# The first half of the second conv matrix by seven block products for eight, its stage ordered by the list scheduler

## Chip, cores, metric

One core of one Trainium2 chip runs the whole kernel. The metric is the device time in microseconds (us), the median of the runs; one more execution was taken with the hardware profiler, and all views of the trace are of that one.

## What is computed

One decoder layer on 256 tokens behind 16 meta tokens (D_MODEL 2048, all float32):

```python
u = rms_norm(h, g_pre_mix)
z_pool, v_conv, g_conv, gate_a, gate_b = split(u @ w_in)
y_a = causal_multiscale_pool(z_pool, w_pool_grp, pool_scale) @ w_pool_out
y_b = conformer_conv(v_conv, g_conv, w_dw, b_dw, conv_ln_g, conv_ln_b) @ w_conv_out
m = sigmoid(gate_a) * y_a + sigmoid(gate_b) * y_b
h = h + rms_norm(m @ w_o, g_post_mix)
f = square(relu(rms_norm(h, g_pre_mlp) @ w_up)) @ w_down
h = h + rms_norm(f, g_post_mlp)
```

The change lies in `@ w_conv_out`: (256 x 1024) by (1024 x 2048).

## The kernel before

**Products in three parts.** Every float32 operand is split into a rounded high part (fp32r, a copy on ScalarE) and the rest (a subtraction on VectorE), and a product is the sum of high x high, high x low and low x high. A weight block is 512 rows by 512 columns, 1 MiB: `raw` (three rooms, filled from the queue of SyncE), `hi` and `lo` (three rooms each). One *block product* is 128 tokens by such a block: 4 row groups x 3 parts = 12 matmuls of 128x512.

**The stages around the change**, in order: gates (L831), the group map of the pool (`acc_grp`), the pool projection (`acc_po`, w_pool_out, eight blocks), the conv projection (`acc_co`, w_conv_out, eight blocks), and the products of w_o. Pool and conv projection run through `project_t`: for each of four column blocks n, two row blocks kc, two token halves t. `fetch` keeps the split two blocks ahead: it opens the next block of the list `stream` (its load goes to SyncE's queue when the room `raw` is free, which is when the split of three blocks earlier is done), splits it when TensorE has left the parts of three blocks earlier, and hands out the oldest.

**Work behind the pool stage.** `pending` is a list of VectorE work with costs, drained between products; `late` holds ScalarE work sent off at the next fetch. In the pool stage they run the LayerNorm's end and swish: `c` ends up as the activations S, and `s_act` gets their high and low parts.

**Behind each conv column block** (`evac_conv`, L938, L939): the accumulated block times sg[1] (the sigmoid of gate_b), plus sg[0] (already times the pool's result), into one of four rooms `mts`; later `feature_steps` transposes it on TensorE (`mt`, L920), and ScalarE and VectorE write the parts into `m` (L924, L927); for the first two column blocks ScalarE also copies it to `A` (L929), from which `sums_of_m` (L952 to L955) makes sums for w_o.

**The w_o stage** already does seven block products for eight in places, and its items are ordered by the class `Plan`: each item names its engine, a cost, what it reads and writes; TensorE's and SyncE's items keep the order written out by hand (`STEPS`, which begins "P2 X02 P1 P5 P3 P6"), the others go by the earliest start, then by the time at which TensorE's planned order needs them. What comes out is a fixed program order for every engine. `early_sums` holds two sums of w_o blocks, made by four transfers on GpSimd's queue (two plain, two that add to what is there, L906), issued when the pool stage is over; P5, P6, P4 and P7 use them. P3's weight block is loaded into a room that sg[1] held (tag s1) and added to the first early sum (L1134). L1118 and L1123 are the split in this stage.

Of the kernel before, what the change touches and what calls it, by code (L numbers as in the profile page):

```python
# [15 lines left out]
P = 128  # L16
CK = 4
# [98 lines left out]
def hybrid_block(ctx: ExitStack, tc: tile.TileContext, ins: dict, out: bass.AP):  # L116
# [127 lines left out]
    def part_tile(tag, n, standing=False):  # L244

        key = f"{tag}{n % 3}"
        room = ready.pop(key) if key in ready else part_room(key, f"{tag}_{n}")
        place = 2 if standing and tag == "hi" else 1
        shift = (place - 1 - 3 * KEYS.index(key)) % 4 * LINE
        return room[:, shift:shift + CK * CW]  # L250

    def open_chunk(loads=None):

        n = at["n"]
        at["n"] += 1
        src, (rows, width) = stream[n]
        raw = raws.tile([P, CK * CW], F32, tag="raw", name=f"raw_{n}")
        hi, lo = (part_tile(tag, at["parts"], n in standing_chunks) for tag in ("hi", "lo"))
        at["parts"] += 1
        flat, (raw, hi, lo) = raw, (t.rearrange("p (k c) -> p k c", k=rows) for t in (raw, hi, lo))  # L260
        if n < FIRST:
            dst = raw.rearrange("p k (h c) -> p k h c", h=2)
            for load in loads or [(slice(i, i + 2), BOTH, nc.sync) for i in range(0, rows, 2)]:
                if callable(load):
                    load()
                    continue
                sl, halves_, queue = load
                for k in range(sl.start, sl.stop):
                    queue.dma_start(dst[:, k, halves_], src[:, k, halves_])
        else:  # L270
            nc.sync.dma_start(raw, src)
        pieces = rows if n < FIRST else 4 if n == FIRST else 1
        k = rows // pieces

        def high(sl, cs):
            nc.scalar.copy(hi[:, sl, cs], raw[:, sl, cs])  # L276

        def low(sl, cs):
            nc.vector.tensor_sub(lo[:, sl, cs], raw[:, sl, cs], f32(hi[:, sl, cs]))  # L279
# [10 lines left out]
        opened.append((hi, lo, todo, flat))  # L290

    def split_pieces(c):
        while opened[c][2]:
# [529 lines left out]
    def block(n):  # L823
        return slice(n * CW, (n + 1) * CW)
# [60 lines left out]
    pending += [(0, ln_out), (0, ln_act)]  # L885

    def evac_pool(n):
        def f(t, acc):
# [11 lines left out]
    def source_o(key):  # L900
        return columns(w_o, key[0] * CK, CK, key[1] * CW)[0][0]

    early_sums = big.tile([P, 2, CK * CW], F32, tag="k8", bufs=2, name="early_sums")
    for keys, op in ((((0, 0), (0, 1)), {}), (((0, 1), (1, 1)), {"accum_op": ALU.add})):
        for e, key in enumerate(keys):
            nc.gpsimd.dma_start(early_sums[:, e].rearrange("p (k c) -> p k c", k=CK),  # L906
                                source_o(key), **op)

    pairs_room = big.tile([P, 3, 2 * T], F32, tag="ux", name="pairs")
    m = big.tile([P, LINE + KD * 2 * T], F32R, tag="um", name="m")[:, LINE:].rearrange(  # L910
        "p (k a t) -> p k a t", k=KD, a=2)

    def feature_steps(n, t, mt):

        box = {}

        def turn():
            box["pt"] = pt = misc_tile(f"mt_{n}_{t}").rearrange("p (k c) -> p k c", k=CK)
            for i in range(CK):
                nc.tensor.transpose(pt[:, i, :], mt[:, i * P:(i + 1) * P], ident)  # L920
        dst = m[:, n * CK:(n + 1) * CK, :, t * P:(t + 1) * P]

        def high():
            nc.scalar.copy(dst[:, :, 0, :], box["pt"])  # L924

        def low():
            nc.vector.tensor_sub(dst[:, :, 1, :], box["pt"], f32(dst[:, :, 0, :]))  # L927
            if n < 2:
                nc.scalar.copy(A[:, t, n], box["pt"])  # L929
        return turn, high, low  # L930

    def mt_of(n, t):
        return mts[:, (n * NT + t) % (CC // CW * 2), :]

    def evac_conv(n):
        def f(t, acc):
            mt = mt_of(n, t)
            nc.vector.tensor_mul(mt, acc, sg[1][:, t, block(n)])  # L938
            nc.vector.tensor_add(mt, mt, sg[0][:, t, block(n)])  # L939
            blocks.extend(feature_steps(n, t, mt))  # L940
        return f

    def s_act_of(k):
        return ln["out"][:, k, :, :]


    A = big.tile([P, NT, 2, CK, P], F32, tag="a", name="A")

    def sums_of_m():

        a11, a12, a21, a22 = (A[:, t, h] for t in range(2) for h in range(2))
# [5 lines left out]
    mts = big.tile([P, CC // CW * 2, CW], F32, tag="c", name="mts")  # L957
    blocks = []
# [7 lines left out]
    later = {}  # L966

    class Norm:

# [50 lines left out]


    plan = Plan()
    HALVES = ("hi", "lo")
# [199 lines left out]

    def m_last(t):

        f_pe, f_hi, f_lo = feature_steps(NB - 1, t, mt_of(NB - 1, t))
# [846 lines left out]
```

## Time and profile before

| | |
|---|---|
| median of 3 runs | 1184.38 us (1184.14 to 1184.66) |
| profiled execution | 1184.32 us |
| its span, first to last instruction | 1182.6 us |
| granted TensorE clock | 0.997 |
| busy: TensorE / VectorE / ScalarE / GpSimd | 1172.7 / 1027.6 / 679.6 / 45.0 us |
| pool projection on TensorE | 333.19 to 376.74 us |
| conv projection on TensorE | 376.74 to 422.99 us |

PE is TensorE, DVE VectorE, ACT ScalarE, POOL GpSimd, SP SyncE. The chain lists, in order of time, what the end of the span hung on: start, us, engine, tile, line, and how many instructions. In the groups, x8 | 18.3, 2289 means eight instructions, 18.3 us in all, 2289 ns each; behind the next bar stands the idle time of the engine just ahead of them and what ended it. A timeline row is start, us, engine, line, operation, out<-in. A row of windows is the stretch, its length, busy time and instructions of the engine asked for, then the granted clock, the DMA engines' busy share, and GB/s.

### The profile page before, as it was taken

The page shows a single profiled execution, that of the slowest core. Times are in us where ns is not written, and L with a number is a line of the kernel's source. Part 1 is how long each engine was busy: PE and PEld are TensorE (multiplying, and loading weights), DVE is VectorE, ACT ScalarE, POOL GpSimd, SP SyncE. Part 2 cuts the span into 40 slices and gives each one's busy share as a digit, 9 for nine tenths or more (in the row PEclk, how much of TensorE's full clock was granted, in tenths as well). Part 3 has the DMA queues.
Part 4 walks back from the last instruction along what each step waited for, and adds up shares of the span by engine and source line. Part 5 has one row for each costly group of instructions (what it writes and reads, how often), then busy time and mean ns, then how long its engine had stood idle before and what let it go on. Part 6 is the DMA issues. An engine that isn't in the chain of part 4 may idle for free.

```text
span 1182.6 us, 15774 instructions
## 1 busy us (share of the span) xinstructions
PE 1172.7 (99%) x6351; PEld 1018.9 (86%) x6351; DVE 1027.6 (87%) x1095; ACT 679.6 (57%) x690; POOL 45.0 (4%) x51
## 2 busy tenths in 40 slices
PE   9999999999999999999999999999999999999997
PEld 9999988888888888898888888888888888888886
DVE  6899978999766799987998988989989989889865
ACT  6533344444584465756566766666656667666642
POOL 1000000000000001000001001000000010010000
PEclk9999999999999999999999999999999999999998
DMA  8655565655647967859869898988998898998861
GB/s 295 214 178 179 182 204 184 196 195 184 208 143 268 265 215 221 290 168 317 248 213 249 228 288 220 269 269 226 281 293 215 267 279 229 282 241 239 303 214 72
DMA packets 177882, 272.91 MB, mean 231 GB/s; under 512 B 4657, under 2 KB 92913, under 8 KB 176912
## 3 DMA queue, kind: packets, MB, share of 16 engines
q1 hardware_dynamic: 160176, 235.88, 59.0%
q0 software_dynamic: 16736, 34.76, 16.2%
q10 hardware_dynamic: 896, 1.25, 0.3%
q8 instruction: 50, 0.82, 0.3%
q14 instruction: 24, 0.20, 0.1%
HBM read 267.68 MB, written 4.19 MB: 230 GB/s over the span
## 4 chain that ended last, share of the span: by engine, by line
PE 99%; DVE 0%; DVEq 0%; issue 0%; ACT 0%; ACTq 0%
PE bank_u L498 18%; PE acc_gate L802 15%; PE bank_a L1787 10%; PE bank_u L504 9%; PE acc_up L1787 8%; PE bank_b L1787 7%; PE o_c L1170 6%; PE acc_z L493 4%; PE acc_co L802 4%; PE acc_po L802 4%; PE acc_v L493 3%; PE acc_g L493 3%; PE acc_vg L493 2%; PE acc_up L498 1%; PE bank_u L1787 1%; PE o_b L1170 1%
## 5 line engine op out<-in xcount | busy, mean ns | idle before, releaser
L498 PE MATMUL bank_u<-m,hi 128*128 128x512 f32 x960 | 329.4, 390 | 0.0
L504 PE MATMUL bank_u<-m,lo 128*128 128x256 f32 x960 | 265.5, 277 | 0.0
L276 ACT CAST hi<-raw 128x2048 fp32r<-128x2048 f32 (+2 forms) x94 | 151.0, 1620 | 188.1 <-PE acc_gate L802 64.0
L498 PEld LDWEIGHTS bank_u<-m,hi 128*128 128x128 f32 x960 | 180.2, 188 | 37.9
L279 DVE TENSOR_TENSOR lo<-raw,hi 128x2048 fp32r<-128x2048 f32 (+2 forms) x94 | 180.0, 1925 | 34.6 <-ACT hi L276 34.1
L1570 DVE TENSOR_TENSOR lo<-raw_m,hi 128x2048 fp32r<-128x2048 f32 x70 | 160.3, 2290 | 31.6 <-ACT hi L1566 31.5
L504 PEld LDWEIGHTS bank_u<-m,lo 128*128 128x128 f32 x960 | 180.3, 188 | 1.4
L1566 ACT CAST hi<-raw_m 128x2048 fp32r<-128x2048 f32 x70 | 133.9, 1912 | 73.7 <-DVE raw_m L1583 21.3
L802 PE MATMUL acc_gate<-hi,u_um 128*128 128x512 f32 x416 | 131.1, 389 | 0.0
L559 DVE SCALAR_TENSOR_TENSOR c<-a,taps,c 128x256 f32<-128x256 f32 x240 | 115.7, 484 | 6.8
L1787 PE MATMUL bank_a<-hi,forms 128*128 128x512 f32 (+1 forms) x288 | 93.5, 386 | 0.0
L802 PEld LDWEIGHTS acc_gate<-hi,u_um 128*128 128x128 f32 x416 | 78.1, 188 | 16.1
L802 PE MATMUL acc_gate<-lo,u_um 128*128 128x512 f32 x208 | 80.9, 389 | 0.0
L1570 DVE TENSOR_TENSOR lo<-raw_a,hi 128x2048 fp32r<-128x2048 f32 x29 | 66.4, 2290 | 10.8 <-ACT hi L1566 10.7
L1566 ACT CAST hi<-raw_a 128x2048 fp32r<-128x2048 f32 x29 | 55.4, 1910 | 35.4 <-PE bank_u L498 13.2
L1566 ACT CAST hi<-raw_c 128x2048 fp32r<-128x2048 f32 x27 | 51.5, 1909 | 27.2 <-PE bank_u L498 12.4
L1570 DVE TENSOR_TENSOR lo<-raw_c,hi 128x2048 fp32r<-128x2048 f32 x27 | 61.8, 2289 | 5.7 <-ACT hi L1566 5.6
L1787 PEld LDWEIGHTS bank_a<-hi,forms 128*128 128x128 f32 x288 | 53.9, 188 | 11.0
L1570 DVE TENSOR_TENSOR fourth_pair<-raw_m,fourth_pair 128x2048 fp32r<-128x2048 f32 x26 | 59.5, 2288 | 4.4 <-ACT fourth_pair L1566 4.4
L1650 ACT COPY half<-bank_u 128x256 f32<-128x256 f32 x60 | 22.2, 370 | 66.0 <-PE bank_u L504 66.0
L1787 PE MATMUL acc_up<-hi,forms 128*128 128x512 f32 x176 | 57.4, 390 | 0.0
L1787 PE MATMUL bank_a<-lo,forms 128*128 128x512 f32 (+1 forms) x144 | 55.6, 386 | 0.0
(419 smaller groups left out, 2265.0 us busy)
## 6 DMA issues: line engine op xcount, KB each, us to landing
raw<-in_w_in_dram SPq DMA_DIRECT2D x52, 1024.0 KB, 5.1
raw_m<-in_w_down_dram SPq DMA_DIRECT2D x38, 1024.0 KB, 7.0
raw_m<-in_w_down_dram POOLq DMA_DIRECT2D x22, 1024.0 KB, 10.6
raw_a<-in_w_up_dram SPq DMA_DIRECT2D x20, 1024.0 KB, 6.4
raw_c<-in_w_up_dram SPq DMA_DIRECT2D x19, 1024.0 KB, 6.9
raw_m<-in_w_up_dram SPq DMA_DIRECT2D x19, 1024.0 KB, 6.9
raw_a<-in_w_down_dram SPq DMA_DIRECT2D x13, 1024.0 KB, 7.3
raw_c<-in_w_down_dram SPq DMA_DIRECT2D x13, 1024.0 KB, 7.3
```

What stands on the lines that cost most here:

```text
L276: nc.scalar.copy(hi[:, sl, cs], raw[:, sl, cs])
L279: nc.vector.tensor_sub(lo[:, sl, cs], raw[:, sl, cs], f32(hi[:, sl, cs]))
L493: nc.tensor.matmul(acc, w[:, k[0], cs], act[:, k[1], a, off:], start=first and n == 0, stop=last and n == 2)
L498: nc.tensor.matmul(acc.rearrange("p (a t) -> p a t", a=2)[:, :, ts], hi[:, k[0], cs], act[:, k[1], :, off + ts.start:off + ts.stop], start ...
L504: nc.tensor.matmul(acc[:, :T], lo[:, k[0], cs], act[:, k[1], 0, off:], start=False, stop=stop, skip_group_check=True)
L559: nc.vector.scalar_tensor_tensor(c, conv["a"][:, q, i:i + T], taps[:, q, i:i + 1], c, op0=ALU.mult, op1=ALU.add)
L802: nc.tensor.matmul(acc, act(kk)[:, a_, ts_], w_[:, k, :], start=kk == 0 and n == 0, stop=kk == nk - 1 and n == 2)
L1170: nc.tensor.matmul(acc, form(k, a_), box[w_][:, k, :], start=start and k == 0 and n == 0, stop=stop and k == CK - 1 and n == 2, skip_group ...
L1566: nc.scalar.copy(box["hi"], raw)
L1570: nc.vector.tensor_sub(box["lo"], raw, f32(box["hi"]))
L1650: nc.scalar.copy(box[j], accs[j][:, :T])
L1787: nc.tensor.matmul(acc, forms[h][:, f, k, a_, :], box[w_][:, k, cs], start=start and k == 0 and n == 0, stop=stop and k == KH - 1 and n == ...
```

## The change

**Seven for eight.** For the first two column blocks (n = 0, 1) the matrix is a 2 x 2 grid of blocks Bkn, the activations a 2 x 2 grid of halves Ath (tokens t, channels h), and four results are made by seven block products on sums. Products 1, 2 and 4 take the plain activations from `s_act`; 5, 6, 7 and 3 take sums of them (`conv_sums`, four passes over c in place, then a high and a low part each, `conv_high`, `conv_low`). On the weight side 1, 2 and 3 take plain blocks; 5 takes B11 + B12, 6 that plus B22, 7 B12 + B22, and 4 the sum of all four. These sums are made in `conv_wide`, in the room of u (tag um), by eight transfers on GpSimd's queue, issued ahead of the pool stage: three plain, five that add; B22 is added to the room of 5 on VectorE, behind the split of 5.

**Column blocks 2 and 3** stay plain: X20, X21, X30, X31 (column block, row block), each for token half a and b. So eight products more.

**Order.** The stage is no longer `project_t` but a second `Plan`, `cplan`. TensorE's order is `ORDER`; f00 is the transposition of column block 0, token half 0; `sums` is sums_of_m. The first two blocks ("1", "5") are still opened and split by the pool stage's fetch. Each of eleven weight entries is split (before: eight). The four results of the seven products are put together from one bank `ch`, to which 1, 6, 7 and 4 are added one after the other, with ScalarE copies of it in between (`keep`), and two more banks; each joined result then takes the two gate passes as before. `mts` gets its room (tag c) only when all forms have been read from c.

**What moves.** `early_sums` is loaded behind product 3, since the forms of 7 and 3 hold its room (tag k8) until then; `m` and `A` get their rooms inside the stage.

```diff
@@ the list of weight blocks
-    for w, nk in ((w_pool_out, KP), (w_conv_out, KC)):
-        for n in range(NB):
-            stream += columns(w, 0, nk, n * CW)
+    for n in range(NB):
+        stream += columns(w_pool_out, 0, KP, n * CW)
...
+    CONV = ("1", "5", "6", "2", "7", "X20", "4", "3", "X21", "X30", "X31")
+    CONV_LOADS = {"1": (0, 0), "2": (1, 0), "3": (1, 1)}
+    ORDER = "1 5 6 2 7 X20a f00 X20b 4 3 f11 X21a f01 X21b f10 sums X30a X30b f20 f21 X31a X31b"
...
+    def open_room(key):
+        raw = conv_raw(key)
+        hi, lo = (part_tile(tag, at["parts"]) for tag in ("hi", "lo"))
...
+        more = conv_raw("3") if key == "5" else None
+        def f():
+            nc.scalar.copy(hi, raw)
+            nc.vector.tensor_sub(lo, raw, f32(hi))
+            if more is not None:
+                nc.vector.tensor_add(raw, raw, more)
...
@@ ahead of the pool stage
-        pending[0:0] = [a_[0], b_[0], FETCH, a_[1], b_[1], FETCH, a_[2], b_[2]]
+        pending[0:0] = [a_[0], b_[0], FETCH, a_[1], b_[1], FETCH, a_[2], b_[2],
+                        (2.4, conv_sums), FETCH] + [(0.6, conv_low(key)) for key in "56"]
...
+    conv_wide = big.tile([P, 3, CK * CW], F32, tag="um", name="conv_wide")
+    sums_ = {"6": ((0, 0), (0, 1)), "7": ((0, 1), (1, 1)), "4": ((0, 0), (0, 1), (1, 1), (1, 0))}
+    for i in range(4):
+        for n, (key, blocks_) in enumerate(sums_.items()):
+            conv_rooms[key] = conv_wide[:, n]
+            if i < len(blocks_):
+                add_into(conv_rooms[key], conv_block(*blocks_[i]), ALU.add if i else None)
...
+    FORM_C = {"5": (0, 0, (1, 0)), "6": (0, 1, (1, 1)), "7": (1, 0, (0, 0)), "3": (1, 1, (0, 1))}
...
@@ behind the pool stage
-    for keys, op in ((((0, 0), (0, 1)), {}), (((0, 1), (1, 1)), {"accum_op": ALU.add})):
-        for e, key in enumerate(keys):
-            nc.gpsimd.dma_start(early_sums[:, e].rearrange("p (k c) -> p k c", k=CK),
-                                source_o(key), **op)
...
-    for n in range(NB):
-        after += blocks + [sums_of_m] * (n == 2)
-        blocks.clear()
-        project_t(s_act_of, KC, evac_conv(n), f"co{n}")
+    cplan = Plan()
+    BANK_C = {"1": "ch", "6": "ch", "7": "ch", "4": "ch", "2": "w2", "5": "w3", "3": "w3"}
...
+    def load_c(e, src, rows=CK, ahead=False):
+        r = n_loads[0] % 3
+        n_loads[0] += 1
+        loads_c[e] = f"raw{r}"
...
+        cplan.add("SP", 0.0 if ahead else 3.1, f, writes=(f"raw{r}",), late=0.0 if ahead else 3.0)
...
+        cplan.add("ACT", 1.83, high, reads=(name,), writes=(f"hi{q}",))
+        cplan.add("DVE", 2.22, low, reads=(name, f"hi{q}"), writes=(f"lo{q}",))
...
+    cplan.add("ACT", 0.0, place_forms, writes=("S7", "S3"))
+    for key in "73":
+        form_parts(key)
...
+    cplan.add("ACT", 0.0, place_mts, writes=["c"] + [f"h{i}" for i in range(4)])
...
+    def keep(n, t, bank):
+        cplan.add("ACT", 0.5, lambda: nc.scalar.copy(mt_of(n, t), conv_banks[bank]),
+                  reads=(bank,), writes=(h_of(n, t),))
...
+        if unit == "1":
+            keep(0, 0, "ch")
+        elif unit == "5":
+            keep(0, 1, "w3")
+        elif unit == "6":
+            keep(1, 0, "ch")
+            cplan.add("ACT", 0.0, place_a, writes=("S5", "S6", "Aroom"))
+        elif unit == "2":
+            joined(0, 0, nc.vector.tensor_add, lambda: conv_banks["w2"], lambda: mt_of(0, 0),
+                   ("w2", h_of(0, 0)))
+        elif unit == "7":
+            keep(1, 1, "ch")
...
+        elif unit == "3":
...
+            cplan.add("ACT", 0.0, place_early, writes=("S7", "S3", "early0", "early1"))
+            early_load(0, (0, 0), None)
+            early_load(1, (0, 1), None)
+            early_load(0, (0, 1), ALU.add)
+            early_load(1, (1, 1), ALU.add)
+        elif unit == "4":
+            gate_conv(0, 1, "ch")
...
+    cplan.emit()
```

More of the change, by code (lines that the diff above doesn't have):

```diff
@@ new lines, in gate_conv, with joined @@
+    def gate_conv(n, t, bank=None):
+        h = h_of(n, t)
+        cplan.add("DVE", 0.62, lambda: nc.vector.tensor_mul(
+            mt_of(n, t), conv_banks[bank] if bank else mt_of(n, t), sg[1][:, t, block(n)]),
+            reads=(bank,) if bank else (h,), writes=(h,))
+        cplan.add("DVE", 0.62, lambda: nc.vector.tensor_add(
+            mt_of(n, t), mt_of(n, t), sg[0][:, t, block(n)]), reads=(h,), writes=(h,))
+    def joined(n, t, op, a_, b_, names):
+        cplan.add("DVE", 0.62, lambda: op(mt_of(n, t), a_(), b_()), reads=names,
+                  writes=(h_of(n, t),))
+        gate_conv(n, t)
@@ new lines, in hybrid_block, with features, steps @@
+    turns = [0]
+    def features(n, t):
+        assert {"mroom", "Aroom"} <= set(cplan.writer)
+        box, bank, j = {}, f"mt{turns[0] % 2}", f"m{n}{t}"
+        turns[0] += 1
+        def steps():
+            if "s" not in box:
+                box["s"] = feature_steps(n, t, mt_of(n, t))
+            return box["s"]
+        cplan.add("PE", 0.45, lambda: steps()[0](), reads=(h_of(n, t),), writes=(bank,))
+        cplan.add("ACT", 0.53, lambda: steps()[1](), reads=(bank, "mroom"), writes=(j,))
+        cplan.add("DVE", 0.62, lambda: steps()[2](), reads=(bank, j), writes=(j + "l",))
+        if n < 2:
+            cplan.add("ACT", 0.5, lambda: nc.scalar.copy(A_[0][:, t, n], box["s"][3]["pt"]),
+                      reads=(bank, "Aroom"), writes=(f"A{t}{n}",))
@@ new lines, in place_early @@
+    def place_early():
+        later["early"] = big.tile([P, 2, CK * CW], F32, tag="k8", bufs=2, name="early_sums")
+    entry_of = {key: e for e, key in enumerate(CONV)}
+    used = {}
+    for u_, unit in enumerate(UNITS):
+        used[entry_of[unit.rstrip("ab")]] = u_
+    W_O = (len(CONV), len(CONV) + 1)
+    BEHIND = {}
+    for item in ORDER.split():
+        if item in UNITS:
+            last_unit = item
+            BEHIND[item] = []
+        else:
+            BEHIND[last_unit].append(item)
@@ new lines, in hybrid_block, with after_split @@
+    loaded = ["2", "X20", "X21", "X30", "X31"]
+    wanted_c = [(entry_of[key], conv_block(*(CONV_LOADS.get(key) or (int(key[2]), int(key[1]))))[0])
+                for key in loaded] + [(W_O[i], stream[at["n"] + len(CONV) - ahead_c + i][0])
+                                      for i in range(2)]
+    n_loads[0] = 2
+    load_c(*wanted_c.pop(0), ahead=True)
+    loads_c[entry_of["1"]], loads_c["3"] = "raw0", "raw1"
+    split_done = ahead_c
+    x_banks = []
+    def after_split(e):
+        if wanted_c and e in (entry_of[k] for k in ("2", "3", "X20", "X21", "X30", "X31")):
+            load_c(*wanted_c.pop(0))
@@ L965, in hybrid_block @@
+    while split_done < len(CONV) + 2:
+        split_c(split_done, "w_o")
+        split_done += 1
+    cplan.emit()
+    m = later["m"]
+    early_sums = later["early"]
+    for e in W_O:
+        opened.append((*conv_parts[e], [], flats[e]))
+    at["parts"] = first_c + len(CONV) + 2
+    at["n"] += len(CONV) - ahead_c + 2
     og = big.tile([P, NT, D], F32, tag="k8", bufs=2, name="og")
-    later = {}
+    A = A_[0]
     class Norm:
@@ L1022, in hybrid_block @@
     plan = Plan()
-    HALVES = ("hi", "lo")
     SA1, SA2, SA3, SA4 = ((1, 0), (1, 1), (0, 0), (0, 1))
```

178 lines of the change are left out of this document (155 added, 23 removed).

## The prediction

> **What bounds the kernel now.** I read the page first (busy times, then the chain that ended last), then the chain between 333 and 462 us, then VectorE's groups and windows there, then the DMA queues.
>
> ```profile
> span 1182.6 us, 15774 instructions
> PE 1172.7 (99%) x6351; PEld 1018.9 (86%) x6351; DVE 1027.6 (87%) x1095; ACT 679.6 (57%) x690; POOL 45.0 (4%) x51
> PE 99%; DVE 0%; DVEq 0%; issue 0%; ACT 0%; ACTq 0%
> ```
>
> TensorE is the bound: it is busy for 99% of the span and the chain runs through it for 99%. A matmul left out shortens the kernel only while nothing makes TensorE wait; VectorE, at 87%, is the engine that could.
>
> ```profile
> 333.19 43.55 PE acc_po L802 x192
> 376.74 16.32 PE acc_co L802 x72
> 393.06 0.87 PE mt L920 x8
> ...
> 422.99 2.73 PE o_c L1170 x12
> 432.05 2.72 PE o_a L1170 x12
> 434.77 5.44 PE o_c L1170 x24
> ```
>
> Three stages follow each other without a gap: the pool projection, the conv projection (376.74 to 422.99, 46.25 us: 192 matmuls and, three times, eight transposes), and w_o. In w_o, P2 stands at 422.99, P1 at 432.05, P5 at 434.77 and P3 behind it at 437.5.
>
> **What it saves.** A block product is 12 matmuls, 2.73 us (16.32/6). The stage had 16 and gets 7 + 8 = 15; the six transposes stay. If nothing waits, the saving is 2.7 us, 0.23% of the time: this is the ceiling, and any stop of TensorE comes off it. About 0.2%, 2.4 us, is what a measurement here can tell from no change.
>
> **What it adds on VectorE.**
>
> ```profile
> L279 DVE TENSOR_TENSOR lo<-raw,hi 128x2048 fp32r<-128x2048 f32 x8 | 18.3, 2289 | 7.6 <-ACT hi L276 7.6
> L939 DVE TENSOR_TENSOR mts<-mts,sg 128x512 f32<-128x512 f32 x7 | 4.8, 692 | 0.2
> 376.74:422.99 46.25, 33.67 (x33) 1.00 0.83 250
> 422.99:462.00 39.01, 37.50 (x29) 1.00 0.87 284
> 373.28 2.29 DVE L279 TENSOR_TENSOR lo<-raw,hi 128x2048 fp32r<-128x2048 f32 x1 [3.15 <-ACT hi L276]
> 375.49 0.69 DVE L889 TENSOR_TENSOR sg<-acc_po,sg 128x512 f32<-128x512 f32 x1
> 371.33 1.91 ACT L276 CAST hi<-raw 128x2048 fp32r<-128x2048 f32 x1 [3.53 <-PE acc_po L802]
> 393.53 0.58 ACT L924 CAST m<-mt 128x512 fp32r<-128x512 f32 x1 [3.96 <-PE mt L920]
> ```
>
> A split costs ScalarE 1.9 and VectorE 2.2 us (start to start, 373.28 to 375.49); a pass over 128x512 costs VectorE some 0.65. Behind the pool stage VectorE now gets eleven splits for eight (24.2), sixteen gate passes (10.4), six low parts (3.9), the sums of m (2.6), and new: two low parts of forms (1.3), three joins (1.95), the tail of B22's addition (1) and the last two pool evacuations (1.3): 46 to 47 us, against 33.67 before. TensorE needs 15 x 2.73 + 2.6 = 43.6. So VectorE turns from a quarter idle into as long as the stage; what it can't finish goes into w_o, where it is busy 37.5 of 39.0 us. The four sums of A (2.5) and the low parts of forms 5 and 6 lie in the pool stage, where VectorE waits 3.15 us before single splits: they cost nothing, and delay the split of the last pool block by under 3 us, which TensorE needs 4 us later.
>
> **The stop at product "6".** ScalarE and VectorE work in program order. "5" is split first; behind its subtraction VectorE adds B22 to the same room; only then "6" can be cast; and TensorE may add "6" to the chain's bank only when ScalarE has kept the bank in mts, whose room is that of c, which the forms 7 and 3 must have left. From the rows: cast of "5" 371.33, subtraction 373.28 to 375.5, addition to 377.7, cast of "6" to 379.6, subtraction to 381.9, two form subtractions to 383.2, the copy (0.58) to 383.8. TensorE gets there at 376.74 + 2 x 2.73 = 382.2. A stop of 1.6 us, then, even if all data are there. The planner counts neither the addition nor the pool evacuations, since both were issued ahead of it.
>
> **What it adds on the queues.** Eight transfers of 1 MiB go to the GpSimd queue as soon as u's room is free: three plain, five that add. Nothing else stands on it there. The early sums of w_o (two and two) move from the start of the stage to behind product "3".
>
> ```profile
> 325.00 0.39 PE L802 MATMUL acc_gate<-hi,u_um 128*128 128x512 f32 x1
> 358.26 34.03 SPq L271 DMA_DIRECT2D raw<-in_w_conv_out_dram  x8
> 377.04 1.57 POOL L906 DMA_DIRECT2D early_sums<-in_w_o_dram  x2 [371.21 <-PE acc_po L802]
> 384.98 1.30 POOL L906 DMA_DIRECT2D early_sums<-in_w_o_dram  x1 [6.37 <-DMA early_sums<-in_w_o_dram]
> 388.50 1.28 POOL L906 DMA_DIRECT2D early_sums<-in_w_o_dram  x1 [2.22 <-DMA early_sums<-in_w_o_dram]
> early_sums<-in_w_o_dram POOLq DMA_DIRECT2D x1, 1024.0 KB, 7.4
> early_sums<-in_w_o_dram POOLq DMA_DIRECT2D x1, 1024.0 KB, 13.5
> early_sums<-in_w_o_dram POOLq DMA_DIRECT2D x1, 1024.0 KB, 18.0
> 381.04 0.37 SPq L271 DMA_DIRECT2D raw<-in_w_conv_out_dram  x1
> raw<-in_w_conv_out_dram SPq DMA_DIRECT2D x1, 1024.0 KB, 5.1
> raw<-in_w_conv_out_dram SPq DMA_DIRECT2D x1, 1024.0 KB, 8.7
> 386.48 0.37 SPq L271 DMA_DIRECT2D raw<-in_w_conv_out_dram  x1
> raw<-in_w_conv_out_dram SPq DMA_DIRECT2D x1, 1024.0 KB, 13.3
> 391.92 0.37 SPq L271 DMA_DIRECT2D raw<-in_w_conv_out_dram  x1
> raw<-in_w_conv_out_dram SPq DMA_DIRECT2D x1, 1024.0 KB, 14.9
> ```
>
> The last column is the time to landing of the load issued in that window. A weight load alone takes 5.1. The loads issued at 381.04, 386.48 and 391.92 landed at 389.7, 399.8 and 406.8; the two adding transfers at 398.5 and 406.5. So while adding transfers are on, one weight block and one adding block pass per (406.7 - 389.7)/2 = 8.5 us, where the stage eats a block per 5.4.
>
> Put on the pool stage: the plain three, shared with loads, end near 332, 338 and 344 (some 5.8 each, two blocks at 2.9); the first three adding ones near 352, 360 and 368. The load of "1", issued at 358.26, stands behind the last pool block (which I put at 364.5) and lands near 370.7 instead of 363.4. Its split ends on VectorE near 374.8, in time for 376.74; the split of "5" then ends at 377.0, the addition (B22 landed at 376.3) at 379.2 instead of 377.7. The stop at "6" grows by 1.5 to 3.2 us (my value: the pair price was measured on these same queues; bounds 1.6, if the loads keep their 5.1, and some 5, if every pair takes the 10.1 of the first one).
>
> The sum of "4" adds three times in a chain, each after the last has landed: two more of 8.5 and two issues, landed near 392. It is cast at the earliest behind product "2"; TensorE needs "4" at 376.74 + 7 x 2.73 + 0.4 + 3.2 = 399.4, so the cast by 395. Cost nothing, 3 us spare; past that every us is TensorE's, and it stands in ScalarE's queue before the copy behind "7", the split of "3" and the features of block (0,0).
>
> For one such transfer the Trainium skill (DMA: Bandwidth & Descriptors, Anatomy of one DMA) gives 2.0 us plus bytes over 436 GB/s, 4.4 us for 1 MiB. Eight in a row would then be done by 361 and the stop at "6" would stay at 1.6; the rows above, 7.4 to 18.0, speak against it.
>
> **The stop in w_o.**
>
> ```profile
> 423.03 1.92 ACT L1118 CAST hi<-raw_o 128x2048 fp32r<-128x2048 f32 x1 [3.00 <-PE acc_co L802]
> 424.98 2.29 DVE L1123 TENSOR_TENSOR lo<-raw_o,hi 128x2048 fp32r<-128x2048 f32 x1
> 431.19 2.28 DVE L1134 TENSOR_TENSOR early_sums<-early_sums,raw_o 128x2048 f32<-128x2048 f32 x1
> 434.07 2.29 DVE L1123 TENSOR_TENSOR lo<-raw_o,hi 128x2048 fp32r<-128x2048 f32 x1
> ```
>
> P3's split ends at 436.3, 1.2 us ahead of TensorE: the tightest place. Its block is loaded when the last gate has left sg's room, and added to the first early sum at 431.19. With the stop of 3.2 the conv stage ends at 376.74 + 43.6 + 3.2 = 423.5, 0.5 later than before. VectorE, full since 381, does the last gate product near 426.4 instead of 424.3. The early transfers start behind "3", at 405; the plain ones land near 413 and 418, the adding ones near 427 and 435 (before: 398.5 and 406.5). P3's load of 426.4 shares with the last of these and lands near 435.3; addition to 437.5, a form to 438.1, the split to 440.4. TensorE wants it at 437.5 + 0.5 = 438.0: a stop of 2.4. Bounds: none, if that load takes 5.1 and lands at 431.5; 5, if it takes the 13 to 15 us of the loads above.
>
> **The sum.** -2.7 + 3.2 + 2.4 = +2.9 us. The profiled execution took 1184.32 for its span of 1182.6 and the median is 1184.38, so I say 1187.2. Everything behind w_o is as before.
>
> **The rivals.**
> - *Only the chain at "6" stops.* Loads land as alone: -2.7 + 1.6, and up to 1 for VectorE's backlog: 1183.2 to 1184.2, within 0.2%. For it: in 325 to 377 the DMA engines now have slack. Against: eight transfers come into it. 0.27.
> - *Nothing stops: the faster side.* If VectorE puts the two form subtractions into its waits before the split of "6" and the copy of the chain's bank leaves before 382.2, and the blocks land alone, the 2.7 stays: 1181.6. It decides at whether "6" starts at 382.2. Against: the order on VectorE is by due time, which puts the split of "6" first. 0.08.
> - *The sum of "4" lands late.* At 10 us a pair the chain lands at 397 to 400; ScalarE and VectorE stand still behind that cast, and since VectorE has no slack it costs 2 to 5 on top: 1189 to 1193. 0.13.
> - *The plan does not say what is run.* The planner names the room of X21's load as that of B22. If the pool of rooms really turned in that order, the load would wait for the split of "3" near 402, land 5 to 8 later, and X21 (wanted at 408) start at 412 to 414: 1191 to 1194. 0.06. For it: the names; against: two other rooms are free earlier.
> - *The clock drops behind a stop.*
>
> ```profile
> 1.12 3.35 PE idle L394 x14
> 5.82 0.67 PE idle L394 x6
> ```
>
> The first fourteen of these small matmuls took 239 ns each, six later ones 112. If a stop of over 3 us brings this back for 3.35 us, half of it, 1.7, is added: 1189. In these windows the granted clock is 1.00 and there is no stop, so the trace can't tell. The Trainium skill (TensorE: Matmul & The Clock Gate, HAM oscillation) has the limit at idle gaps of about 3.4 us. 0.05.
>
> **Chances and range.** Forecast 0.41. Slower: the forecast and the last three, 0.65, less some 0.04 for the forecast's lower half, which falls under 2.4: 0.61. Faster 0.08. Within 0.2%: 0.31. The range takes in the quiet rival and its neighbour, from 1182.0, and reaches over the late "4" and the room, to 1194.0; the likeliest case's own range, by the bounds of both stops, is 1183 to 1191.
>
> **What would show it.** Right: a TensorE gap of 2 to 4 us before the third product of the conv stage, released by ScalarE's copy of the chain's bank; weight loads of 8 us and more between 344 and 410; VectorE over 95% busy from 381 to 425; a second gap at the fifth product of w_o, behind the addition to the first early sum. Wrong: loads of 5 us in the pool stage (then the first stop is 1.6 and the second is gone); no gap at "6"; or the longest gap at "4" or X21.

## The result, and the profile after

The changed kernel takes 1187.92 us (median of seven executions, 1186.58 to 1188.65) against 1184.55 for the kernel before (seven, 1183.91 to 1184.72): ratio 1.0029, 95% interval 1.0017 to 1.0041. It is slower, by 3.4 us. Its profiled execution took 1186.58, the shortest of the seven; so the profile below accounts for 2.3 of the 3.4 us, and the rest has to be looked for elsewhere.

The page after, the share of the chain, and TensorE's waits from the pool stage on (engine, line, what ended the wait; us in total, times, longest):

```profile
span 1184.9 us, 15791 instructions
PE 1171.5 (99%) x6339; PEld 1016.4 (86%) x6339; DVE 1042.9 (88%) x1110; ACT 689.6 (58%) x701; POOL 53.9 (5%) x59
PE 92%; DVE 3%; DMA 3%; ACT 1%; issue 0%; DVEq 0%; ACTq 0%
PE acc_co_chain L1205 <- ACT mts L1095: 2.6, 1, 2.6
PE o_c L1459 <- DVE lo L1412: 0.6, 1, 0.6
PE acc_po L844 <- DVE lo L293: 0.6, 1, 0.6
```

Twelve matmuls fewer, and the chain, which ran through TensorE for 99%, now leaves it for two long stretches (338.5 to 385.5 and 400.0 to 439.7). TensorE's three waits lie in these; the chain shows what it passes through ahead of each:

```profile
342.80 19.30 DMA raw<-in_w_pool_out_dram
...
366.45 10.41 DMA raw_conv<-in_w_conv_out_dram
376.96 2.30 DVE conv_wide L318
379.36 1.91 ACT hi L1054
381.30 1.07 DVE lo L1058
383.51 1.30 DVE conv_forms L962 x2
384.83 0.59 ACT mts L1095
385.47 3.02 PE acc_co_chain L1205 x12
...
401.92 2.29 DVE lo L1058
...
425.89 0.61 DVE mts L1100
426.52 7.95 DMA raw_o<-in_w_o_dram
434.56 2.29 DVE early_sums L1423
437.45 2.21 DVE lo L1412
439.71 2.81 PE o_c L1459 x11
```

First place, the pool stage: the load of its last-but-one block takes 19.3 us, and TensorE stands still until 366.5. Second, product "6": B22's block lands at 376.9, then addition, cast, subtraction, the two forms, ScalarE's copy of the chain's bank, and only then "6". Third, P3 in w_o: its load is issued only at 426.52, behind the conv stage's gate passes, and from 401.9 to there the chain runs through VectorE with gaps of no more than 0.7; then the block lands at 434.5, and addition and split follow. Measured from the start of the last matmul ahead to the start of the second one behind, less the 0.23 that each of the two takes in a row, the stops are 0.84, 2.83 and 0.86 (the rows of waits above read 0.27 less), and the eight transpositions at 426.7 take 0.30 longer than before: 4.83 in sum. With the saved block product, -2.73 + 4.83 = +2.1 of the span's +2.3.

VectorE between the start of the conv stage and its last gate pass, and three of the transfers (the last number is us from issue to landing: the first three adding ones into the sums, issued at 332.5, 336.5 and 340.2):

```profile
377.30:426.52 49.22, 46.75 (x44) 1.00 0.83 248
conv_wide<-in_w_conv_out_dram POOLq DMA_DIRECT2D x1, 1024.0 KB, 15.2
conv_wide<-in_w_conv_out_dram POOLq DMA_DIRECT2D x1, 1024.0 KB, 20.1
conv_wide<-in_w_conv_out_dram POOLq DMA_DIRECT2D x1, 1024.0 KB, 24.4
```

VectorE is busy for 46.75 of 49.22 us, in a stage for which TensorE alone would need 43.6.

### The profile page after: what moved, and what is told of

The parts are those of the page before. It is cut to its first block, busy times and chain, and to the rows that moved or that the text cites. A ratio compares the mean times of both kernels' runs of the same rounds, so it can differ in the third digit from the quotient of the medians.

```text
span 1184.9 us, 15791 instructions
## 1 busy us (share of the span) xinstructions
PE 1171.5 (99%) x6339; PEld 1016.4 (86%) x6339; DVE 1042.9 (88%) x1110; ACT 689.6 (58%) x701; POOL 53.9 (5%) x59
## 4 chain that ended last, share of the span: by engine, by line
PE 92%; DVE 3%; DMA 3%; ACT 1%; issue 0%; DVEq 0%; ACTq 0%
PE bank_u L540 18%; PE acc_gate L844 15%; PE bank_a L2076 10%; PE bank_u L546 9%; PE acc_up L2076 8%; PE bank_b L2076 7%; PE o_c L1459 5%; PE acc_z L535 4%; PE acc_v L535 3%; PE acc_g L535 3%; PE acc_vg L535 2%; DMA raw<-in_w_pool_out_dram 2%; PE acc_up L540 1%; DVE lo L1058 1%; PE bank_u L2076 1%; DMA raw_conv<-in_w_conv_out_dram 1%
## 5 line engine op out<-in xcount | busy, mean ns | idle before, releaser
L290 ACT CAST hi<-raw 128x2048 fp32r<-128x2048 f32 (+2 forms) x85 | 134.0, 1589 | 178.4 <-PE acc_gate L844 64.0
L293 DVE TENSOR_TENSOR lo<-raw,hi 128x2048 fp32r<-128x2048 f32 (+2 forms) x85 | 159.4, 1886 | 26.0 <-ACT hi L290 25.6
L1859 DVE TENSOR_TENSOR lo<-raw_a,hi 128x2048 fp32r<-128x2048 f32 x29 | 66.4, 2288 | 10.8 <-ACT hi L1855 10.7
```

Of the source, the lines that this page charges most:

```text
L1859: nc.vector.tensor_sub(box["lo"], raw, f32(box["hi"]))
```

## The experiments

Four theories. **T**: the stops are made by late data and by the chain behind the split of "6"; take one cause away, and its stop goes. **V**: VectorE, with 46 us of work in a stage of 43.6, is the bound itself; a stop taken away comes back further on. **P**: the order of the work behind "5" makes the stop at "6" by itself, whenever data come. **C**, formed after the first traces: the granted clock falls behind the stop in some executions, not in the profiled one. All times are medians; "over" is the difference to the kernel before in the same set of runs (for the changed kernel +3.37). The intervals reach 1.0 to 1.7 us to either side, and only that of none_of_three lies clear of the changed kernel's (1.0017 to 1.0041): the smaller gains rest on the traces, which show what stop went and what stop came.

| run | median us | over | ratio's 95% interval |
|---|---|---|---|
| no_adding_sums | 1186.33 | +2.27 | 1.0012 to 1.0032 |
| no_b22 | 1185.52 | +1.46 | 1.0002 to 1.0019 |
| no_early_adds | 1187.36 | +3.30 | 1.0016 to 1.0038 |
| none_of_three | 1182.69 | -1.37 | 0.9980 to 0.9997 |
| two_before_six | 1186.79 | +2.80 | 1.0014 to 1.0032 |
| four_from_six | 1187.56 | +3.57 | 1.0019 to 1.0044 |
| both_orders | 1187.88 | +3.89 | 1.0020 to 1.0045 |
| before_plus_transfers | 1187.89 | +3.90 | 1.0020 to 1.0046 |
| filled_stop | 1187.23 | +2.88 | 1.0014 to 1.0034 |
| six_by_transfers | 1188.08 | +3.73 | 1.0023 to 1.0051 |
| bank_kept_early | 1185.75 | +2.04 | 1.0008 to 1.0026 |
| early_and_four_from_six | 1186.15 | +2.44 | 1.0012 to 1.0029 |

### One cost taken away at a time, then all

**no_adding_sums**

```diff
-            if i < len(blocks_):
+            if i < 1:
```

> The three sums of weight blocks get their plain transfer only; the five adding ones are left out, so 5, 6, 7 and 4 are computed from unsummed blocks (the addition of B22 on VectorE stays). Theory T (the adding transfers delay the weight loads, and these set the stops): the weight loads of the pool stage's end and of 1 and B22 land after 5 to 8 us for 10 to 19, the stop of 0.8 at the pool stage's last-but-one block goes, the stop before product 6 shrinks from 2.8 to about 1.6; 1.7 to 2.2 us less than the changed kernel. Rival V (VectorE, with 46 us of work in a stage of 43.6, is itself the bound): the stop at 6 stays at 2.5 to 3 whatever the loads do, and the time moves by under 0.8. Rival P (the order behind 5 alone: addition, cast, subtraction, forms, copy): 6 stays at 2.5 or more, only the pool stage's stop goes, 0.8 less.

One row of the chain, then TensorE's waits:

```profile
332.93 38.12 PE acc_po L844 x168
PE acc_co_chain L1205 <- ACT mts L1095: 1.9, 1, 1.9
PE mt L991 <- DVE mts L1103: 0.7, 1, 0.7
```

The pool stage runs without a stop, as T said. The wait at "6" shrinks from 2.6 to 1.9; by the measure of the stops above that is 2.20 for 2.83, where T said 1.6 and P 2.5 or more. A new wait of 0.7 at a transposition, behind VectorE's gate pass, has come, and the gain is 1.1, where T said 1.7 to 2.2 and P 0.8. In this trace B22 lands at 369.1, well ahead of its addition at 375.3, and still "6" stops for 2.2 us: the order behind "5" makes that much by itself, nearer to P's number than to T's. Late data had put off the end of this chain by 1.6 us (385.4 for 383.8), but TensorE's coming too, by 1.0, by way of the pool stage, so only 0.6 of it showed in the stop. The adding transfers are a cause, of the pool stage's stop above all.

**no_b22**

```diff
-            if more is not None:
-                nc.vector.tensor_add(raw, raw, more)
```

> Leaves out VectorE's addition of B22 to the room of 5, so 6 is computed from the sum for 5. All transfers stay. T: the cast of 6 no longer waits for B22's load (landed 376.9) nor for the 2.3 us of the addition, the stop at 6 goes from 2.8 to 0.6 or less; the pool stage's 0.8 and P3's 0.9 stay; about 2.2 us less than the changed kernel. V: 2.3 us less on VectorE give the stage 2.3 us too, but by way of the whole stage, so that the stop in w_o goes as well. P: as T.

```profile
PE o_a L1457 <- DVE m L998: 0.9, 1, 0.9
PE acc_co_chain L1203 <- ACT mts L1093: 0.7, 1, 0.7
PE mt L989 <- DVE mts L1101: 0.6, 1, 0.6
```

These are TensorE's waits again. The one at "6" falls from 2.6 to 0.7 (as a stop 0.98, where T said 0.6 or less); 1.9 are gained. Yet with 2.3 us less work VectorE now holds TensorE up at two places where it didn't before: P1 in w_o (0.9, behind the low part of m) and a transposition (0.6). P3's stop is gone, as V said and T didn't. That speaks for V as a second limit right behind the first.

**no_early_adds**

```diff
-            early_load(0, (0, 1), ALU.add)
-            early_load(1, (1, 1), ALU.add)
```

> Leaves out the two adding transfers into the early sums of w_o (their plain ones stay), so w_o's products on these sums use unsummed blocks. T: P3's load of 426.5 lands after 5 to 6 us for 8.0, near 432, the stop of 0.9 at the fifth product of w_o goes; 0.9 to 1.2 less than the changed kernel, and the stops at the pool stage and at 6 stay. V: VectorE gets to P3 no earlier, since it is full from 377 on; the stop stays at 0.6 to 0.9 and the time is unchanged within 0.3.

The chain at "6", then TensorE in windows of 4 us (length, busy time, matmuls, granted clock, DMA share, GB/s):

```profile
386.20 4.51 PE acc_co_chain L1205 x12
384.00:388.00 4.00, 1.80 (x4) 0.75 0.72 131
388.00:392.00 4.00, 4.00 (x16) 0.82 0.77 248
```

The wait of P3 is gone from the list, as T said, but the time is that of the changed kernel within the intervals, so T's 0.9 to 1.2 was not gained (V's number, but not V's stop: that one did go). The profiled execution shows something of its own: behind a wait of 2.60 at "6" the granted clock falls, and the product takes 4.51 us where it took 3.02. The clock lost in these two windows is 4 x 0.25 + 4 x 0.18 = 1.7 us, more than the stop at P3 could give back.

**none_of_three**: the three edits above together.

> All three left out together: the five adding transfers into the sums of the conv stage, VectorE's addition of B22, and the two adding transfers into the early sums. T: all stops of TensorE between 325 and 462 are gone or under 0.3 in sum, and what is left is the saved block product: 2.3 to 2.7 us below the kernel before, 1181.7 to 1182.3. V or anything else that the steps do not name (a longer time for the matmuls, the clock, work behind w_o): it stays over 1183.5.

```profile
PE acc_co_chain L1203 <- ACT mts L1093: 0.7, 1, 0.7
PE mt L989 <- DVE mts L1101: 0.3, 1, 0.3
376.80:425.00 48.20, 45.09 (x44) 1.00 0.50 175
```

1.37 below the kernel before, 4.74 below the changed one. The three alone gave 1.10, 1.91 and 0.07, 3.1 together: a stop that goes lets another come, and in the profiled execution of no_early_adds the clock took the gain back. It stays 0.4 to 1.0 short of T's 1181.7 to 1182.3, and V's "over 1183.5" is missed by more: "6" still waits 0.7 for the copy of the bank, and VectorE (last line), at 45.09 of 48.20 us, sets the end of the stage with a wait of 0.3. As stops these are 0.97 and 0.36, and -2.73 + 1.33 = -1.4 is what was measured. The executions lie within 1.2 us, those of the kernel with everything in it within 2.1.

### Transfers alone

**before_plus_transfers**: the kernel before, with the eight transfers.

```diff
+    conv_wide = big.tile([P, 3, CK * CW], F32, tag="um", name="conv_wide")
...
+                nc.gpsimd.dma_start(conv_wide[:, n].rearrange("p (k c) -> p k c", k=CK),
+                                    columns(w_conv_out, kb * CK, CK, nb * CW)[0][0],
+                                    **({"accum_op": ALU.add} if i else {}))
```

> The kernel before, full computation, with the eight transfers of the conv sums added ahead of its pool stage on GpSimd's queue; nobody reads what they make. Nothing else is changed, its early sums' four transfers now queue behind them. T: the loads late in the pool stage and early in the conv stage land after 10 to 19 us and TensorE stops for 0.8 at the pool stage's last-but-one block, and the early sums start only when the chain of 4's sum is through (387 for 377), which puts P3's load of 425 beside them: 1 to 2.5 us slower than the kernel before. V and P: transfers alone cost nothing, within 0.5 of the kernel before.

One row of the chain, and three from TensorE's timeline (what ended the idle time stands in brackets):

```profile
342.89 19.60 DMA raw<-in_w_pool_out_dram
366.86 0.50 PE L802 MATMUL acc_po<-lo,y 128*128 128x512 f32 x1 [0.85 <-DVE lo L279]
406.55 0.63 PE L930 MATMUL mt<-ident,mts 128*128 128x128 f32 x4 [0.63 <-DVE mts L949]
421.05 0.63 PE L930 MATMUL mt<-ident,mts 128*128 128x128 f32 x4 [0.70 <-ACT m L934]
```

Eight transfers that nobody reads cost the old kernel 3.9 us, more than T's 1 to 2.5, and as much as the whole change. The pool stage's load is late by the same amount (19.6), and in the conv stage VectorE's splits wait for late loads, behind them its gate passes, and behind these the transpositions. V, which priced them at nothing, fails here: the transfers are a cost of their own. But 3.9 isn't their share in the change. Only the first stop (1.1) stands in the changed kernel too; the other four (2.7 together) come behind loads that took 12 to 18 us beside the early sums, which here queue behind the eight. In the changed kernel the early sums start at 405.7, and the conv stage's loads from 387 on take 5.1.

### Other orders, the whole computation kept

**two_before_six**

```diff
-    CONV = ("1", "5", "6", "2", "7", ...
+    CONV = ("1", "5", "2", "6", "7", ...
```

with the same swap in `ORDER`.

> Full computation. Only TensorE's order changes: 1 5 2 6 7 for 1 5 6 2 7, in the list of weight entries and in the order of products. T: one more block product (2.73) lies between 5 and 6, so the stop of 2.8 before 6 falls under 0.3; in its place 2 waits for its load (issued behind the last of the four, landed near 379 to 380, split to 384) against 382.2: a new stop of 0 to 2. Net 1 to 2.5 us less than the changed kernel, the pool stage's 0.8 and P3's 0.9 stay. V: VectorE has the same work, the stop turns up again later in the stage (at 7, 4 or X21) and the time stays within 0.5. P: 2.5 less.

```profile
PE acc_co_chain L1205 <- ACT mts L1095: 1.5, 2, 0.8
PE mt L991 <- DVE mts L1103: 1.4, 2, 0.7
PE o_a L1459 <- DVE m L1000: 0.9, 1, 0.9
PE acc_co L1205 <- DVE lo L1058: 0.9, 1, 0.9
```

The wait of 2.6 has broken into six smaller ones of 0.7 to 0.9, beside the pool stage's: at "2" by T, at "6", where T had said under 0.3, and at "7", the transpositions and P1 by V. 0.6 gained, T's lower end missed. (The trace is of the longest of eleven executions, 1188.30.)

**four_from_six**

```diff
-             "4": ((0, 0), (0, 1), (1, 1), (1, 0))}
...
+    conv_rooms["4"] = conv_rooms["6"]
...
+            if key == "6":
+                cplan.add("POOL", 5.6, lambda: add_into(conv_rooms["6"], conv_block(1, 0)), ...)
```

> Full computation. The sum of 4 is made from the room of 6 by one adding transfer of B21 behind the split of 6, in place of a room of its own with one plain and three adding transfers: five transfers on GpSimd's queue for eight, three of them (two plain ones among them) less in the pool stage. T: the loads at the pool stage's end land after 8 to 12 us for 13 to 19, its stop goes, B22 lands 1 to 2 us earlier and the stop at 6 falls to 1.6 to 2; about 1.5 to 2 less than the changed kernel. 4 is in time if its one adding transfer takes 10 (issued near 383, landed near 394). V and P: the stop at 6 stays at 2.5 or more; only the pool stage's 0.8 goes.

```profile
PE acc_co_chain L1210 <- ACT mts L1097: 1.9, 1, 1.9
384.46 4.60 PE acc_co_chain L1210 x12
384.00:388.00 4.00, 3.54 (x10) 0.68 0.82 125
388.00:392.00 4.00, 4.00 (x17) 0.89 1.09 263
```

The pool stage's stop is gone, by T, and the wait at "6" is 1.9 (as a stop 2.20, where T said 1.6 to 2); but behind these 1.9 us the clock falls here too (third and fourth line: 4 x 0.32 + 4 x 0.11 = 1.7 us lost), the product takes 4.60, and nothing is gained.

**both_orders**: these two edits together.

> Full computation; the two edits together: 2 ahead of 6, and the sum of 4 from the room of 6. T: pool stop gone, no stop at 6, under 1 at 2; P3's 0.9 stays: 3 to 3.8 below the changed kernel, about 1184, so the same as the kernel before or up to 0.8 faster. The sum of 4 now starts one product later (its room is free behind the split of 6 near 385) and lands near 396, needed by 395: up to 1.5 may come back there. V: within 0.8 of the changed kernel.

```profile
PE acc_co_chain L1210 <- DVE lo L1060: 2.4, 1, 2.4
```

The expectation failed where it had put a caution: "4" now waits 2.4 us, since its last transfer starts only behind the split of a "6" that itself comes later (issued at 384.9, landed at 393.5). "6" and "7" wait for 1.2 more. Nothing gained.

**six_by_transfers**

```diff
+    sums_ = {"5": ((0, 0), (0, 1)), "6": ((0, 0), (0, 1), (1, 1)), "7": ((0, 1), (1, 1))}
...
-                nc.vector.tensor_add(raw, raw, more)
```

and the sum of "4" from the room of "6", the block of "3" loaded behind that of X20.

> Full computation. The sum of 6 is made by transfers (one plain, two adding) in a room of its own and the sum of 4 by one more adding transfer into that room behind the split of 6; VectorE's addition of B22 goes (2.3 us), eight transfers on GpSimd's queue as before, and the block of 3 is loaded only behind that of X20. T: 6 waits for the copy of the chain's bank only until about 382.5 to 383, a stop of 0.7 or less as without the addition; the pool stage's stop stays at 0.6 to 0.8; 2.2 to 2.6 us less than the changed kernel, 1185.3 to 1185.7. V: VectorE's shorter work shows as stops of 0.5 to 0.9 elsewhere (the transpositions, P1 in w_o), as without the addition, so not under 1185. If the sum of 4 lands late (its last transfer can only start behind the split of 6, some 380, and has to land by 395), a stop of 1 to 2 before 4 takes it back.

```profile
358.85 15.71 DMA raw<-in_w_conv_out_dram
PE acc_po L840 <- DVE lo L293: 2.4, 2, 1.8
PE acc_co_chain L1206 <- ACT mts L1092: 0.7, 1, 0.7
```

At "6" it does about what was said (0.7 for 2.6). But the fourth addition is now issued at 357.1, for 364.9, beside the pool stage's last load (16.5 us for 12.8) and that of "1" (15.7 for 10.1), and the pool stage stops for 2.4. The 2.3 us taken from VectorE have been put on the DMA queues.

### The clock

**filled_stop**

```diff
+            if unit == "5":
+                for i in range(8):
+                    nc.tensor.matmul(conv_banks["w2"], form(i % CK, 0), hi[:, i % CK, :],
+                                     start=True, stop=True, skip_group_check=True)
```

> Full computation, the changed kernel with eight more matmuls of 128x512 behind product 5 (8 x 0.227 = 1.8 us, into the bank of 2, which 2 starts anew), inside the stop of 2.8 before 6. Theory C (in most executions the clock falls behind that stop, for three windows some 1.5 us dearer, as the traces of two other runs show and that of the changed kernel does not): the stop left is 1.0, the clock stays at 1.00 in every execution, the median falls by 1.0 to 1.5 to 1186.4 to 1186.9, and the executions lie within 1. Rival (the spread has another cause, as DMA traffic): median and spread as before, 1187.5 to 1188.3; if the eight matmuls delayed 6, slower.

```profile
PE acc_co_chain L1205 <- ACT mts L1095: 0.8, 1, 0.8
384.00:388.00 4.00, 3.24 (x14) 1.00 0.68 124
```

The wait is 0.8 and the clock 1.00, and the extra matmuls cost nothing. The gain over the changed kernel is 0.5, half of the least that C said, the nine executions still lie 1.9 apart (1185.99 to 1187.85), and the intervals overlap.

The mean clock that was granted to each execution says more. In the fourteen traces the last 3.5 to 6.7 us of the program run at half clock, which takes 0.0015 to 0.0028 off the mean; a fall takes 0.0014 more. So a mean of 0.998 or 0.999 holds no fall, 0.996 holds one, and 0.997 may be either. All nine executions of filled_stop stand at 0.998: C's condition is met in each, and they spread all the same. Of the changed kernel's seven, the one at 0.999 took 1187.88, the one at 0.996 1188.30. Where falls come they do cost: in four_from_six the three executions at 0.996 took 1187.54 to 1187.62, the one at 0.998 1186.41. C explains single executions; it doesn't explain the spread, and that it explains the changed kernel's median is not shown.

### The room of the copy

**bank_kept_early**

```diff
-            keep(0, 0, "ch")
+            cplan.add("ACT", 0.5, lambda: nc.scalar.copy(pairs_room[:, 0, :], conv_banks["ch"]),
+                      reads=("ch",), writes=("p0",), late=1.6)
```

> Full computation. ScalarE keeps the chain's bank of product 1 in a room that is free (of the pairs, tag ux) instead of in mts, whose room the forms 7 and 3 must leave first; the copy now stands behind the casts of 6's block and the forms, ahead of the cast of 2. T (the stop at 6 is a chain of waits behind the split of 6): 6 waits only for its own split, which ended at 383.6 in the changed kernel; the stop falls from 2.8 to 0.9 to 1.2, the clock stays up, 1.9 to 2.6 less than the changed kernel: 1185.3 to 1186.0. V (VectorE is the bound whatever 6 waits for, since its work is unchanged): the 1.9 come back as stops between 395 and 430, at the transpositions, 4 or P1 in w_o; less than 1 gained.

```profile
PE mt L991 <- DVE mts L1103: 1.0, 2, 0.7
PE o_a L1460 <- DVE m L1000: 0.9, 1, 0.9
PE acc_co L1205 <- DVE lo L1058: 0.4, 1, 0.4
PE acc_co_chain L1205 <- DVE lo L1058: 0.3, 1, 0.3
```

With addition and transfers all in place, the wait at "6" falls from 2.6 to 0.3 (last line; as a stop from 2.83 to 0.83). In the changed kernel the copy left at 384.83, behind the forms (384.80), whose room it needed, and behind the cast of "2" on ScalarE (384.1); the split of "6" had ended at 383.6. This run takes away both, since the copy now also stands ahead of that cast; of the two, the room was the later. The gain is 1.3, between T's 1.9 and V's 1; the rest of the 2.3 came back behind VectorE, at the transpositions, P1 and "2". (The profiled execution, 1187.26, is the second longest of eleven.) So T names the stop rightly, and V what replaces it.

**early_and_four_from_six**: with the edit of four_from_six as well.

> Full computation: the same early copy, together with the sum of 4 made from the room of 6 (five transfers for eight). T: no stop in the pool stage, the split of 6 ends near 382.6, PE wants it at 382.4: a stop under 0.5 at 6, no lower clock; left are some 0.4 at 4, 0.3 at the transpositions and 0.3 to 0.5 in w_o, and the saved block product's 2.7 stands against them: 1183.4 to 1184.6, so within 0.1% of the kernel before, perhaps below it. V: VectorE, full from 377 to 425 (46 us of work for 43.6), ends the conv stage as late as in the other runs; stops of 1.5 to 2 in sum turn up behind 395, 1185 to 1186.

```profile
PE o_a L1465 <- DVE m L1002: 1.8, 1, 1.8
411.94 14.10 DMA raw_o<-in_w_o_dram
```

No stop in the pool stage and none at "6"; instead "2" and "4" wait 0.4 each and P1 in w_o 1.8, behind a chain whose head is w_o's own load, 14.1 us on its way. 1186.15, no better than bank_kept_early, near V's numbers and not T's. No kernel that does the whole work beats the one before.

## Why the prediction was right, and where it was not

1187.2 was forecast, 1187.92 measured, on the side that was named. By its steps:

*Ceiling, -2.7.* Holds: a block product takes 2.72 to 2.73 in the changed kernel too.

*VectorE, 46 to 47 us.* Measured 46.75, 95% of the window. The prediction used this only to place the last gate and P3. The experiments show that it weighs more: the rival "only the chain at 6 stops" allowed up to 1 us for the backlog and came to 1184.2 at most, while no_adding_sums, close to that case, stays 2.3 over the kernel before (1.2 in its profiled execution, in which the clock didn't fall).

*The stop at "6", 3.2.* Measured 2.83, and the chain named step by step is the one in the trace: B22 landed at 376.9 (376.3 said), the addition ended at 379.25 (379.2), the cast at 381.3, the copy at 385.4. What the stop is short of 3.2 is TensorE's coming later (382.75 for 382.2), held up in the pool stage. bank_kept_early, where the copy needs no room of mts and stands earlier, has a stop of 0.83: the end of this chain held "6". With the data in time (no_adding_sums) the chain ends at 383.8, with late data at 385.4, both as forecast; what differs is when TensorE comes, at 381.8 and 382.75. The step is right in its links, and shown.

*The transfers.* The pair price of 8.5 fits the spacing of the adding transfers, which landed at 347.7, 356.6 and 364.6, each some 4 us earlier than said, as the plain three were done at 339.9 for 344; the sum of "4" was complete at 387.1 for 392, and its cost of nothing holds. The step that failed is that the prediction followed only the load of "1" through this traffic and took the pool stage's own blocks as in time: one of them took 19.3 us, and TensorE stopped for 0.84 there. That these transfers cost something by themselves is shown by before_plus_transfers. Of the signs named, loads of 8 us and more held only until 383.5; from 387 on, with the sum of "4" complete, the conv stage's loads took 5.1. VectorE was busy for 95.8% of 381 to 425, as said.

For the single transfer, the Trainium skill (DMA: Bandwidth & Descriptors, Anatomy of one DMA) gave 4.4 us by its 2.0 us plus bytes over 436 GB/s; the five adding ones here took 10.8 to 24.4 from issue to landing, with loads and, the first three, each other beside them. The measurement decides: that formula prices no transfer that adds under load.

*The stop in w_o, 2.4.* Mis-sized: 0.86. P3's block landed at 434.5 for 435.3, the split ended at 439.66 for 440.4, and TensorE came by 0.8 later, having stopped in the pool stage. The term left out makes up for part of the term overrated (0.84 + 0.86 against 2.4), so the sum was better than its parts. That is less luck than it looks: as long as TensorE stops at P3, the time is set by the end of P3's split, and a stop further ahead only shortens that one.

*The sum.* +2.9 said for the profiled execution, +2.26 measured on it (1186.58 against 1184.32). The median lies 1.3 above that execution. The prediction had no term for a spread between executions; in single executions part of it is its own rival of the clock (below), the rest is open. So that the median came within 0.7 of 1187.2 is in part luck.

*Rivals.* Only the chain at "6": fell, since the loads were late and P3 stopped too. Nothing stops: fell. The sum of "4": no wait there, but in both_orders, where its last transfer starts later, 2.4, so the mechanism exists. X21's room: fell, since that load is issued at 387.0, ahead of the split of "3" at 396.9. The clock: the price, 1.7, was right to the tenth, the condition, a stop of over 3 us, was wrong.

What stays open: why the executions of the changed kernel lie 2.1 us apart. None_of_three's lie 1.2 apart, filled_stop's 1.9, with no fall of the clock in any. Transfers spread the times without the clock: three executions of before_plus_transfers at a mean of 0.999 took 1186.81, 1187.89 and 1189.41, while the fifteen of the kernel before beside them lie 1.3 apart. Which load is late in which execution a single trace can't show.

## What to carry to other kernels

Before work is moved off the bound engine, add up what it puts on the next one for that stage: here 2.7 us saved on TensorE stood against 13 us more on VectorE, which then had little slack, so that of each stop taken away a part came back in pieces of 0.3 to 0.9 behind it. Transfers that nobody waits for aren't free: put them alone into the old kernel and measure them. And where TensorE waits for a copy, look at what the copy waits for: the longest stop here hung on the room it wrote to and on its place in ScalarE's order, and a free room with an earlier place took most of it away.

## What the hardware showed that was not expected

A stop of 1.93 us (four_from_six) and one of 2.60 (no_early_adds) brought the granted clock down, while one of 2.56 (the changed kernel) and another of 1.93 (no_adding_sums) did not. Both falls stood at 0.50 for 3.41 to 3.42 us, 1.7 us of clock, and made the product 1.5 to 1.6 us longer. So it isn't the length of the stop alone that decides.

Where the stop lies in time decides too. Between two changes of the clock there is, in each of the fourteen traces, a whole multiple of 3.413 us (in no_early_adds 111, 1 and 232 times). Count such steps from the first change that the trace holds: in the step that ended with the fall TensorE was busy for 1.48 us (four_from_six) and 1.02 (no_early_adds), and the fall at the end of the program comes behind a step with 1.50 or less in every trace. No step that the clock came through at full speed has less than 1.67 (both_orders). The stop of the changed kernel was cut by the end of a step at 384.04, with 2.27 and 1.99 us busy in the two. The Trainium skill (TensorE: Matmul & The Clock Gate, What's actually happening) describes a free-running window of 3413 ns and two states, half and full clock: length and depth of both falls agree with that. Its warning (HAM oscillation) is of gaps over some 3.4 us; these traces show the fall behind two shorter ones.

An adding transfer slows more than itself: a weight load that took 5.1 us alone took 8.7 to 19.6 beside such traffic, on another queue. Plain transfers do it too: 11.3 us beside the three plain ones of no_adding_sums.
